# A two-layer hybrid decoder trunk: the RG-LRU recurrence as hand-ordered slots

## The chip, the cores and the metric

The kernel runs on one core of a Trainium2 chip. The metric is the device time of one execution in microseconds (us); a time is the median over its runs. Engines are named as in the profile: PE is TensorE (matrix products; PEld its weight loads), DVE is VectorE, ACT is ScalarE, POOL is GpSimd, SP is SyncE, which here only issues DMAs.

## The reference

One sequence of 1024 positions, width 1024, two layers, float32 throughout. Every layer is `x + gate(c) * mixer(RMSNorm(x) * (1 + scale(c)) + shift(c))`; shift, scale and gate come from one product of silu(c) with `ada_w`. Layer 0 mixes by attention (sliding window of 128 with sinks and relative bias, and forgetting attention). Layer 1 is the Griffin block that most of the change is about:

```python
def rglru_mixer(h, w_in, conv_w, conv_b, w_a, b_a, w_x, b_x, lam, w_out):
    proj = h @ w_in
    xr, gate = proj[..., :LRU_WIDTH], proj[..., LRU_WIDTH:]
    xp = jnp.pad(xr, ((0, 0), (CONV_WIDTH - 1, 0), (0, 0)))      # CONV_WIDTH = 4
    xc = conv_b
    for j in range(CONV_WIDTH):
        xc = xc + xp[:, j:j + S] * conv_w[j]
    # 8 blocks of 128 channels, block-diagonal
    r = sigmoid(einsum('bsnw,nwv->bsnv', xblk, w_a) + b_a)
    i = sigmoid(einsum('bsnw,nwv->bsnv', xblk, w_x) + b_x)
    log_a = -LRU_C * r * softplus(-lam)                           # LRU_C = 8
    a = exp(log_a)
    u = sqrt(-expm1(2.0 * log_a)) * (i * xc)
    # scan over positions: state = a_t * state + u_t
    y = hs * silu(gate)
    return y @ w_out
```

A final RMSNorm ends the trunk.

## The kernel before

Activations stand transposed: 128 channels on the partitions, positions along the free axis, in two halves (h = 0, 1) of 512. Every large product is made in three parts to keep float32 accuracy: weights and activations are each split into a rounded high part (`whi`, `xhi`) and the rest (`wlo`, `xlo`), and `gemm` (line 325) adds whi x xhi, wlo x xhi and whi x xlo in one PSUM bank. A 128-channel output tile of one half is thus 8 x 3 = 24 matrix products of 128x512. Splitting a raw weight half (128x512) is one ACT copy and one POOL subtraction (`split`, line 293); raw halves come by DMA from SP into three buffers.

All instructions go through the helper at line 86, so every row of the profile has L86 and the tiles tell operations apart. A planner outside the kernel orders the instructions of each engine; for engines named in the set `ordered` it keeps the program's order instead. `ordered` holds all engines up to line 609 and PE alone from 610 to line 1298; after that it is empty.

The steps that the change touches, in order of time:
- First norm, second half (lines 508 to 521). `rstd_of` (line 256) makes 1/rms from squares summed on PE into `psq`: DVE and ACT (a Sqrt) make `vb`, and `spread` transposes it on PE into the bank `rs`. `gate_first(i)` takes a gate product out of PSUM (`sg`, a Sigmoid on ACT, then `gy`, a product on DVE).
- Ada products (`mod_steps`, line 542): each is one DVE reduction over a 128x1024 row block that a DMA has brought. Twenty are made with the gates of the second half, two after the last gate, one after each of eight `ps_v` tiles, two at the end.
- `log1p_exp_neg_abs` (line 154), a softplus from Exp and Ln: for the forget gate (line 640), and, at line 1308, for lambda.
- `Chain` (line 1204): the second norm, one object per half: `sums`, `spread` and four `pair`s that write h1 (high and low). Chain 0 is fed in between the products of the first output projection (`ps_o0c`, line 1271), chain 1 in the first lx product (line 1296).
- The recurrence. Channel block c needs the products lx_c (input of the convolution) and lg_c (gate). `use_x` copies lx from PSUM to `xr` and starts `xc`; `recurrence` makes the three other taps on DVE from `xr`, splits `xc` into `xch` and `xcl`, multiplies by the r and i gate matrices (12 products), and makes `th`, `a`, `a2` (in a tile with xcl's tag, so in its buffer), the square root and the scan `hs`; `use_g` gates the result into `y1h`, `y1l`. Program order per c: recurrence(c), lx_{c+2}, lg_c; the planner is free to change it. Outputs alternate between two pairs of PSUM banks (`ps_1`), so a bank comes round every fourth output.
- The second output projection (line 1428) runs its first three tiles over k = 0 to 6 ahead of the last channel's y1.

## Time and profile before

| | |
|---|---|
| median of 3 runs | 904.58 us (901.8 to 905.53) |
| profiled execution | 901.91 us |
| its span, first to last instruction | 900.1 us |
| mean granted clock of TensorE in it | 0.989 |
| busy: PE, DVE, ACT, POOL | 857.3, 599.9, 537.7, 387.8 us |

The page gives busy time by engine, the span in 40 slices and the costliest groups of instructions. In a row of a timeline stand the start in us from the span's first instruction, the duration in us, the engine, the line, the operation, the tiles it writes and reads (`out<-in`), its shape and a count; in square brackets the idle time of the engine ahead of it, and who ended it. Stages, by the tiles: first norm and gates to about 77 us, the rest of the input projections and the attention to about 533, the first output projection to 576, lx, lg and the recurrence to about 812, the second output projection and the final norm to 900.

### The profile page before, as it was taken

To read this page: it belongs to the slowest core of one execution; us is meant where nothing else is said; L and a number is where in the kernel's file an instruction comes from. 1 tells how busy PE (TensorE), PEld (TensorE's weight loads), DVE (VectorE), ACT (ScalarE), POOL (GpSimd) and SP (SyncE) were. 2 spreads that over 40 slices of the span, in tenths; PEclk is the share of its full clock that TensorE was granted. 3 is DMA by queue.
4 is the path that set the end of the run, shared out by engine and by line. 5 is a ranking of instruction groups with operands and counts; after the bars stand their busy time and mean duration, and the time that the engine had idled before them with its cause. 6 is when DMAs were issued, how large, how long until landed. Compare 5 with 4: busy or idle time off the path is not lost.

```text
span 900.1 us, 13512 instructions
## 1 busy us (share of the span) xinstructions
PE 857.3 (95%) x4618; PEld 726.6 (81%) x4618; DVE 599.9 (67%) x1118; ACT 537.7 (60%) x1047; POOL 387.8 (43%) x428
## 2 busy tenths in 40 slices
PE   9999999999999999999989999999999999499995
PEld 8777898888878888888778787788888777387995
DVE  7876797688676565665756677276977788643353
ACT  5745124788676566665756656277757666675332
POOL 4843432343342232332554546353745554686010
PEclk9999999999999999999999999999999999799998
DMA  9944883100013322433464563411111111126042
GB/s 348 403 159 153 275 305 82 49 24 23 26 58 105 121 86 84 125 93 90 143 215 119 161 213 119 131 45 41 42 42 50 53 35 46 35 66 216 1 148 87
DMA packets 54334, 103.84 MB, mean 115 GB/s; under 512 B 6929, under 2 KB 20689, under 8 KB 53497
## 3 DMA queue, kind: packets, MB, share of 16 engines
q1 hardware_dynamic: 53112, 101.93, 34.3%
q10 hardware_dynamic: 1152, 1.05, 0.5%
q8 instruction: 36, 0.59, 0.3%
q14 instruction: 34, 0.27, 0.1%
HBM read 94.02 MB, written 8.93 MB: 114 GB/s over the span
## 4 chain that ended last, share of the span: by engine, by line
PE 64%; DVE 14%; ACT 11%; issue 5%; POOL 3%; DMA 3%; SPq 0%; DVEq 0%; POOLq 0%; ACTq 0%
PE ps_fill L86 21%; PE ps_o L86 8%; PE pst L86 6%; PE ps_o0c L86 5%; PE ps_lx L86 4%; PE oB L86 4%; PE ptB L86 3%; PE sB L86 3%; ACT L86 2%; DVE xc_r L86 2%; DVE ada L86 2%; DVE hs_r L86 2%; DVE th_r L86 2%; PE sA L86 2%; DMA ada<-in_ada_dram 1%
## 5 line engine op out<-in xcount | busy, mean ns | idle before, releaser
L86 DVE TENSOR_TENSOR ptl_B<-ptB,pth_B 128x512 fp32r<-128x512 f32 (+1 forms) x80 | 50.8, 635 | 39.8 <-ACT pth_B L86 39.5
L86 PE MATMUL ps_o<-y1h,wo 128*128 128x256 f32 (+1 forms) x336 | 75.3, 319 | 0.0
L86 ACT ACTIVATE pth_B<-ptB 128x512 fp32r<-128x512 f32 (+1 forms) x80 | 44.1, 552 | 46.0 <-PE ptB L86 45.9
L86 ACT ACTIVATE pB<-pB,mnB 128x128 f32<-128x128 f32 (+3 forms) x64 | 49.6, 774 | 30.7 <-DVE mnB L86 25.2
L86 POOL TENSOR_SCALAR_AFFINE_SELECT pB<-pB 128x128 f32<-128x128 f32 x64 | 19.3, 301 | 94.9 <-DMA pB<-gd 85.8
L86 PEld LDWEIGHTS ps_o<-y1h,wo 128*128 128x128 f32 x336 | 55.9, 190 | 4.6 <-issue 0.3
L86 PE MATMUL pst<-hh,ws 128*128 128x512 f32 x192 | 55.5, 397 | 1.5 <-DVE gy L86 1.5
L86 ACT ACT_TABLE_LOAD x42 | 53.9, 1283 | 1.7 <-PEq L1539 0.7
L86 PE MATMUL ps_o<-y1l,wo 128*128 128x256 f32 (+1 forms) x168 | 53.7, 320 | 0.0
L86 DVE CUSTOM_DVE_ANT_0 ada<-ada,crow,col 128x1024 f32<-128x1024 f32 x32 | 46.0, 1467 | 6.9 <-DMA ada<-in_ada_dram 6.8
L86 PE MATMUL ps_lx<-h1h,wlo_lx 128*128 128x512 f32 x128 | 50.1, 393 | 0.4 <-POOL wlo_lx L86 0.4
L86 PE MATMUL ps_lg<-h1h,wlo_lg 128*128 128x512 f32 x128 | 49.9, 390 | 0.2 <-POOL wlo_lg L86 0.2
L86 PE MATMUL ps_lx<-h1l,whi_lx 128*128 128x512 f32 x128 | 49.9, 391 | 0.0
L86 PE MATMUL ps_lx<-h1h,whi_lx 128*128 128x512 f32 x128 | 49.9, 391 | 0.0
L86 PE MATMUL ps_lg<-h1l,whi_lg 128*128 128x512 f32 x128 | 49.8, 389 | 0.0
L86 PE MATMUL ps_lg<-h1h,whi_lg 128*128 128x512 f32 x128 | 49.8, 389 | 0.0
L86 PE MATMUL ptB<-ident,pB 128*128 128x128 f32 x288 | 45.4, 274 | 3.0 <-DVE gy L86 1.2
L86 PEld LDWEIGHTS ptB<-ident,pB 128*128 128x128 f32 x288 | 35.6, 140 | 14.6 <-ACT pB L86 2.3
L86 DVE CUSTOM_DVE_ANT_0 pB<-sB,pB 128x384 f32<-128x384 f32 (+2 forms) x64 | 35.4, 554 | 17.0 <-PE sB L86 8.0
L86 PEld LDWEIGHTS pst<-hh,ws 128*128 128x128 f32 x192 | 35.7, 188 | 10.9 <-DVE gy L86 1.9
L86 ACT ACTIVATE sq_o<-x 128x512 f32<-128x512 f32 (+1 forms) x33 | 18.0, 547 | 38.1 <-DVE x L86 37.9
L86 DVE SCALAR_TENSOR_TENSOR xc_r<-xr_r,col,xc_r 128x1024 f32<-128x1024 f32 x24 | 37.7, 1582 | 1.3 <-ACT xc_r L86 1.0
(317 smaller groups left out, 2856.5 us busy)
## 6 DMA issues: line engine op xcount, KB each, us to landing
ada<-in_ada_dram SPq DMA_DIRECT2D x36, 512.0 KB
ada<-in_ada_dram SPq DMA_DIRECT2D x6, 1024.0 KB
x<-in_xT_dram SPq DMA_DIRECT2D x20, 256.0 KB
pB<-gd SPq DMA_DIRECT2D x8, 512.0 KB
raw_o0a<-in_wo_dram SPq DMA_DIRECT2D x16, 256.0 KB
raw_o0c<-in_wo_dram SPq DMA_DIRECT2D x16, 256.0 KB
x1d<-x SPq DMA_DIRECT2D x16, 256.0 KB
raw_lx<-in_wl_dram SPq DMA_DIRECT2D x16, 256.0 KB
```

The source lines that it names most:

```text
L86: ins = issue(*args, **kw)
```

## The change

The recurrence becomes a list of slots, one for each channel block, with all engines in program order. lx is no longer copied to `xr`: the taps read the PSUM bank itself, and the three positions that the second half needs of the first are kept in `xt`. Weight halves are loaded one by one (`load_next`) and split a tile at a time (`split_next`). Within a slot the ACT functions are put so that sigmoids and tanh, exp, and sqrt stand together. a2 has a tile of its own and is an ACT square; i x xc moves from POOL to DVE; the cut of `xc` moves from DVE to ACT; the subtraction for the gate matrices moves from DVE to POOL. Before the recurrence: `rstd_of` of the first norm's second half stands after three gates instead of ahead of them, two ada products move into the `ps_v` loop, the softplus of lambda moves to the forget gate's, and the steps of both chains move to later products.

```diff
-    spread = rstd_of(psq, HALF, at, ("ptl", "pth"), "n0_1", ps_t)
     for i in range(3):
         gate_first(i)
+    spread = rstd_of(psq, HALF, at, ("ptl", "pth"), "n0_1", ps_t)
...
-        elif i == 7:
-            mod_steps(2)
...
-        mod_steps(1)
-    mod_steps(2)
+        mod_steps(1 + tb % 2)
...
+    log1p_exp_neg_abs(sp, lam, const, [P, KT], "lm")
...
-            parts = {AT_S: chains[0].sums}
+            parts = {5: chains[0].sums}
         elif e == 2:
-            parts = {0: chains[0].spread, 2: lambda: chains[0].pair(0), 6: lambda: chains[0].pair(2)}
+            parts = {3: chains[0].spread, 5: lambda: chains[0].pair(0)}
         elif e == 3:
-            parts = {2: lambda: chains[0].pair(4), 6: lambda: chains[0].pair(6)}
+            parts = {k: lambda k=k: chains[0].pair(k) for k in (2, 4, 6)}
...
-    ps01.append(proj1(0, "lx_0", 0, w01[0], parts={3: chains[1].sums, 6: chains[1].end}))
-    ps01.append(proj1(1, "lx_1", 0, w01[1]))
+    ps01.append(proj1(0, "lx_0", 0, w01[0], parts={3: chains[1].sums}))
+    ps01.append(proj1(1, "lx_1", 0, w01[1], parts={0: chains[1].end}))
...
+    def split_next():
+        if raws:
+            w = []
+            for _ in range(2):
+                w += half_of(raws.popleft())
+                load_next()
+            ready.append(w)
...
+    def conv(c, h, ps):
+
+        if h == 0:
+            xcs[c], xts[c] = rt("xc", c, bufs=2), rt("xt", c, w=3, bufs=2)
+        xc, o = xcs[c], h * HALF
+        act.activation(xc[:, half(h)], ps, AF.Identity, bias=at_c(C_CB, c), scale=at_c(C_CW + 24, c))
+        if h == 0:
+            copy(xts[c], ps[:, HALF - 3 : HALF])
+
+        def taps():
+            for j in range(3):
+                d = 3 - j
+                parts = [(xc[:, o + d : o + HALF], ps[:, 0 : HALF - d])] + [(xc[:, o : o + d], xts[c][:, 3 - d : 3])] * h
+                for out, src in parts:
+                    dve.scalar_tensor_tensor(
+                        out=out, in0=src, scalar=at_c(C_CW + 8 * j, c), in1=out, op0=ALU.mult, op1=ALU.add
+                    )
+
+        return taps
+
+    def split_xc(c, hs=slice(0, S)):
+        if c not in split_x:
+            split_x[c] = rt("xch", c, F32R), rt("xcl", c, F32R)
+        hi, lo = split_x[c]
+        copy(hi[:, hs], xcs[c][:, hs])
+        sub(dve, lo[:, hs], xcs[c][:, hs], r32(hi[:, hs]))
...
+    def split_r(c):
+        for raw, hi, lo in wrs[c].values():
+            copy(hi, raw)
+            sub(gp, lo, raw, r32(hi))
+
+    def gates(c):
...
+            for h, ps in enumerate(out[t]):
+                for i, (a, b) in enumerate(((whi, xch), (wlo, xch), (whi, xcl))):
+                    mm(ps, a, b[:, half(h)], start=(i == 0), stop=(i == 2))
+        return out
+
+    def gate_a(c, h):
+
+        sg = sgs[c, h] = rp.tile([P, HALF], F32, tag="sg", name=f"sg_r{c}_{h}", bufs=2)
+        act.activation(sg, lgs[c, h], AF.Sigmoid)
+        mul(dve, sg, lgs[c, h], sg)
+        mul(gp, sg, sg, hss[c][:, half(h)])
+
+    def gate_b(c, h):
+        sg = sgs.pop((c, h))
+        copy(y1h[:, c, half(h)], sg)
+        sub(gp, y1l[:, c, half(h)], sg, r32(y1h[:, c, half(h)]))
+
+    lgs, sgs = {}, {}
+    ordered |= ALL
+    for _ in range(3):
+        load_next()
+    load_r(0)
+    for c in range(2):
+        conv(c, 0, ps01[c])()
+    split_xc(0, half(0))
+    split_r(0)
+    taps = conv(0, 1, proj1(0, "lx_0", 1, w01[0]))
+    split_next()
+    taps()
+    split_xc(0, half(1))
+    conv(1, 1, proj1(1, "lx_1", 1, w01[1]))()
+
+    def slot(c):
+        n = c + 2
+        ps = gates(c)
+        if c:
+            gate_a(c - 1, 1)
+        r, i_ = rt("r", c), rt("i", c)
+        for o, t, cb in ((r, "r", C_BA), (i_, "i", C_BX)):
             for h in range(2):
...
+                act.activation(o[:, half(h)], ps[t][h], AF.Sigmoid, bias=at_c(cb, c))
+        th, a_, a2 = rt("th", c), rt("a", c), rt("a2", c)
         act.activation(th, r, AF.Tanh, scale=sp[:, c : c + 1])
+        mul(dve, i_, i_, xcs[c])
+        if c + 1 < KT:
+            load_r(c + 1)
+            split_xc(c + 1)
+        if c:
+            gate_b(c - 1, 1)
         act.activation(a_, r, AF.Exp, scale=nsp[:, c : c + 1])
+        w = ready.popleft()
+        split_next()
+        if n < KT:
+            taps = conv(n, 0, proj1(0, f"lx_{n}", 0, w))
+        act.activation(a2, a_, AF.Square)
+        if n < KT:
+            taps()
         dve.scalar_tensor_tensor(out=th, in0=a2, scalar=1.0, in1=th, op0=ALU.add, op1=ALU.mult)
         act.activation(th, th, AF.Sqrt, bias=tiny)
         mul(dve, i_, i_, th)
         hs_ = hss[c] = rt("hs", c, bufs=2)
         dve.tensor_tensor_scan(out=hs_, data0=a_, data1=i_, initial=0.0, op0=ALU.mult, op1=ALU.add)
+        if n < KT:
+            conv(n, 1, proj1(0, f"lx_{n}", 1, w))()
+            w = ready.popleft()
+            split_next()
+        if c + 1 < KT:
+            split_r(c + 1)
+        lgs[c, 0] = proj1(0, f"lg_{c}", 0, w)
+        gate_a(c, 0)
+        gate_b(c, 0)
+        lgs[c, 1] = proj1(0, f"lg_{c}", 1, w)
...
+    gate_a(KT - 1, 1)
+    gate_b(KT - 1, 1)
+    ordered.clear()
```

## Rows read from the trace of the kernel before

**Rows 1.** The page: busy us and share of each engine; TensorE's granted clock by slice.
```profile
PE 857.3 (95%) x4618; PEld 726.6 (81%) x4618; DVE 599.9 (67%) x1118; ACT 537.7 (60%) x1047; POOL 387.8 (43%) x428
...
PEclk9999999999999999999999999999999999799998
```

**Rows 2.** Table by stage: stretch, length, busy us of each engine, clock, DMA share, GB/s.
```profile
714.60:741.20 26.60, 25.08 (x109) 20.06 (x108) 20.06 (x14) 17.90 (x26) 14.62 (x10) 1.00 0.15 45
...
767.80:790.00 22.20, 10.58 (x39) 7.89 (x38) 15.22 (x11) 16.25 (x24) 13.40 (x9) 0.77 0.12 36
```

**Rows 3.** Waits of PE, whole span: us in total, times, longest.
```profile
PE psr L86 <- DVE xcl_r L86: 14.1, 4, 10.3
...
PE ps_v L86 <- DVE fz L86: 1.4, 1, 1.4
```

**Rows 4.** Timeline of PE, a steady pass.
```profile
715.31 0.39 PE L86 MATMUL ps_lg<-h1h,whi_lg 128*128 128x512 f32 x1
...
725.96 0.39 PE L86 MATMUL ps_lg<-h1l,whi_lg 128*128 128x512 f32 x1
...
728.15 0.50 PE L86 MATMUL psr<-xcl_r,wrh_r 128*128 128x512 f32 x1 [1.35 <-DVE xcl_r L86]
...
733.88 0.50 PE L86 MATMUL ps_lx<-h1h,wlo_lx 128*128 128x512 f32 x1 [0.17 <-POOL wlo_lx L86]
```

**Rows 5.** Timeline of PE, the last channel and the second output projection.
```profile
768.34 0.39 PE L86 MATMUL ps_lg<-h1l,whi_lg 128*128 128x512 f32 x1
...
781.31 0.79 PE L86 MATMUL psr<-xcl_r,wrh_r 128*128 128x512 f32 x1 [10.29 <-DVE xcl_r L86]
...
784.40 0.40 PE L86 MATMUL psi<-xch_r,wrh_r 128*128 128x512 f32 x1
...
812.13 0.50 PE L86 MATMUL ps_o<-y1l,whi_wo 128*128 128x512 f32 x1 [1.23 <-POOL y1l L86]
```

**Rows 6.** Timelines of PE, first norm and both chains of the second.
```profile
59.82 0.72 PE L86 MATMUL pst<-hh,ws 128*128 128x512 f32 x2 [1.52 <-DVE gy L86]
...
543.25 0.66 PE L86 MATMUL rs_n<-ident,vb_n 128*128 128x128 f32 x4 [1.37 <-DVE vb_n L86]
...
584.38 0.63 PE L86 MATMUL rs_n<-ident,vb_n 128*128 128x128 f32 x4 [1.81 <-DVE vb_n L86]
```

**Rows 7.** Timeline of ACT, one pass.
```profile
741.08 1.26 ACT L86 ACTIVATE r_r<-psr,col 128x512 f32<-128x512 f32 x2
...
744.16 1.28 ACT L86 ACT_TABLE_LOAD   x1
745.46 1.15 ACT L86 ACTIVATE a_r<-r_r,nsp 128x1024 f32<-128x1024 f32 x1
...
754.56 0.76 ACT L86 ACTIVATE xc_r<-ps_lx,col 128x512 f32<-128x512 f32 x1
755.23 0.62 ACT L86 ACTIVATE whi_lg<-raw_lg 128x512 fp32r<-128x512 f32 x1
```

**Rows 8.** Groups by shape, 560 to 830 us: busy us, mean ns | idle before.
```profile
L86 POOL TENSOR_TENSOR sg_r<-sg_r,hs_r 128x512 f32<-128x512 f32 x16 | 21.3, 1331 | 16.9 <-DVE sg_r L86 10.4 <-DVE hs_r L86 6.6
...
L86 DVE SCALAR_TENSOR_TENSOR th_r<-xcl_r,th_r 128x1024 f32<-128x1024 f32 x8 | 17.1, 2138 | 0.1
...
L86 DVE TENSOR_TENSOR sg_r<-ps_lg,sg_r 128x512 f32<-128x512 f32 x16 | 11.0, 685 | 14.3 <-POOL wlo_lg L86 13.1 <-ACT sg_r L86 1.2
...
L86 DVE SCALAR_TENSOR_TENSOR x<-ps_o0c,mod,x 128x512 f32<-128x512 f32 x4 | 3.0, 751 | 10.3 <-PE ps_o0c L86 10.3
```

**Rows 9.** Timelines of DVE and POOL, two passes.
```profile
626.07 1.22 DVE L86 SCALAR_TENSOR_TENSOR th_r<-xcl_r,th_r 128x1024 f32<-128x1024 f32 x1
...
635.21 2.28 DVE L86 TENSOR_TENSOR_SCAN hs_r<-a_r,i_r 128x1024 f32<-128x1024 f32 x1
...
729.29 1.30 POOL L86 TENSOR_TENSOR wlo_lx<-raw_lx,whi_lx 128x512 fp32r<-128x512 f32 x1 [3.53 <-ACT whi_lx L86]
729.38 3.35 DVE L86 TENSOR_TENSOR_SCAN hs_r<-a_r,i_r 128x1024 f32<-128x1024 f32 x1
```

More of the change, by code (lines that the diff above doesn't have):

```diff
@@ L24 @@
 RUN = 32
-AT_S = 5
 P = 128
@@ L641, in hybrid_trunk @@
     dve.scalar_tensor_tensor(out=lf, in0=z, scalar=0.0, in1=lf, op0=ALU.min, op1=ALU.subtract)
+    sp, nl, nsp = (const.tile([P, KT], F32, name=n) for n in ("sp", "nl", "nsp"))
+    lam = col[:, C_LAM : C_LAM + 8]
+    log1p_exp_neg_abs(sp, lam, const, [P, KT], "lm")
+    dve.tensor_scalar(out=nl, in0=lam, scalar1=-1.0, scalar2=0.0, op0=ALU.mult, op1=ALU.max)
+    add(dve, sp, sp, nl)
+    dve.tensor_scalar(out=nsp, in0=sp, scalar1=-8.0, scalar2=None, op0=ALU.mult)
+    dve.tensor_scalar(out=sp, in0=sp, scalar1=8.0, scalar2=None, op0=ALU.mult)
     gd = dram.tile([8, NB, S], F32, name="gd")
@@ L1320, in hybrid_trunk @@
         jobs_l += [(c + 2, f"lx_{c + 2}")] * (c + 2 < KT) + [(8 + c, f"lg_{c}")]
-    jobs_l = collections.deque(jobs_l)
-    ready = collections.deque()
-    def next_weights():
-        if jobs_l:
-            ready.append(load_tile(wl[jobs_l[0][0]], jobs_l[0][1]))
-            jobs_l.popleft()
-    def proj_l(name, use):
-        next_weights()
-        w = ready.popleft()
-        for h in range(2):
-            use(h, proj1(0, name, h, w))
+    halves = collections.deque((ti, i, name) for ti, name in jobs_l for i in range(2))
@@ L1361, in load_r @@
             sync.dma_start(raw, src[:, c])
-            wrs[c][t] = rt("wrh", c, F32R, w=P, bufs=2), rt("wrl", c, F32R, w=P, bufs=2)
-            copy(wrs[c][t][0], raw)
-            sub(dve, wrs[c][t][1], raw, r32(wrs[c][t][0]))
-    def recurrence(c):
-        xr, xc = xrs[c], xcs[c]
-        for j in range(3):
-            dve.scalar_tensor_tensor(
-                out=xc, in0=xr[:, j : j + S], scalar=col[:, C_CW + 8 * j + c : C_CW + 8 * j + c + 1], in1=xc,
-                op0=ALU.mult, op1=ALU.add,
-            )
-        xch, xcl = rt("xch", c, F32R), rt("xcl", c, F32R)
-        dve.tensor_copy(xch, xc)
-        sub(dve, xcl, xc, r32(xch))
-        ri = []
-        for src, cb, t in ((wa, C_BA, "r"), (wx, C_BX, "i")):
-            whi, wlo = wrs[c][t]
-            o = rt(t, c)
-            for h in range(2):
-                hs = slice(h * HALF, (h + 1) * HALF)
-                ps = (ps_s if t == "r" else ps_t)(f"ps{t}_{c}_{h}")
-                for i, (a, b) in enumerate(((whi, xch), (wlo, xch), (whi, xcl))):
-                    pe.matmul(ps, a, b[:, hs], start=(i == 0), stop=(i == 2))
-                act.activation(o[:, hs], ps, AF.Sigmoid, bias=col[:, cb + c : cb + c + 1])
-            ri.append(o)
-        r, i_ = ri
-        th, a_, a2 = rt("th", c), rt("a", c), rt("xcl", c)
-        act.activation(th, r, AF.Tanh, scale=sp[:, c : c + 1])
-        act.activation(a_, r, AF.Exp, scale=nsp[:, c : c + 1])
-        mul(dve, a2, a_, a_)
@@ new lines, in load_r @@
+            wrs[c][t] = raw, rt("wrh", c, F32R, w=P, bufs=2), rt("wrl", c, F32R, w=P, bufs=2)
+    def split_r(c):
[3 more added lines that the diff above has]
+    def gates(c):
+        out = {}
+        for t, ps_ in (("r", ps_s), ("i", ps_t)):
+            _, whi, wlo = wrs[c][t]
+            xch, xcl = split_x[c]
+            out[t] = [ps_(f"ps{t}_{c}_{h}") for h in range(2)]
+            for h, ps in enumerate(out[t]):
+                for i, (a, b) in enumerate(((whi, xch), (wlo, xch), (whi, xcl))):
+                    mm(ps, a, b[:, half(h)], start=(i == 0), stop=(i == 2))
+        return out
@@ L1398, in recurrence @@
         dve.tensor_tensor_scan(out=hs_, data0=a_, data1=i_, initial=0.0, op0=ALU.mult, op1=ALU.add)
-    def use_g(c):
-        def use(h, ps):
-            hs = slice(h * HALF, (h + 1) * HALF)
-            sg = rp.tile([P, HALF], F32, tag="sg", name=f"sg_r{c}_{h}", bufs=2)
-            act.activation(sg, ps, AF.Sigmoid)
-            mul(dve, sg, ps, sg)
-            mul(gp, sg, sg, hss[c][:, hs])
-            copy(y1h[:, c, hs], sg)
-            sub(gp, y1l[:, c, hs], sg, r32(y1h[:, c, hs]))
-        return use
-    for c in range(2):
-        use = use_x(c)
-        use(0, ps01[c])
-        use(1, proj1(c, f"lx_{c}", 1, w01[c]))
-    next_weights()
-    load_r(0)
-    for c in range(KT):
-        recurrence(c)
-        if c + 1 < KT:
-            load_r(c + 1)
-        if c + 2 < KT:
-            proj_l(f"lx_{c + 2}", use_x(c + 2))
-        proj_l(f"lg_{c}", use_g(c))
+        if n < KT:
[8 more added lines that the diff above has]
+        lgs[c, 1] = proj1(0, f"lg_{c}", 1, w)
+    for c in range(KT):
+        slot(c)
+    gate_a(KT - 1, 1)
+    gate_b(KT - 1, 1)
+    ordered.clear()
     l1.close()
```

34 lines of the change are left out of this document (10 added, 24 removed).

## The prediction

> **What bounds the kernel now.** I read the busy table and the slices first. TensorE (PE) is busy for 857.3 of 900.1 us, and its clock stands at full speed in all slices but two [rows 1], so only what makes PE wait, or makes it run at less than full speed, can move the end. In a dense stretch a 128x512 product follows the last one after (725.96 - 715.31) / 47 = 0.2266 us [rows 4]; that is my yardstick, and a larger step between two products is a loss. The table by stage then shows the recurrence. One pass of its loop (channels 1 to 5) needs 48 products of lx, 48 of lg and 12 of the r and i gates: 108 x 0.2266 = 24.5 us. The stretch of 26.6 us in [rows 2] is such a pass, with DVE at 20.1, ACT at 17.9 and POOL at 14.6 us: no engine beside PE is full, so the 2.1 us above the yardstick are order, not work. The last passes are far worse: from 767.8 to 790.0 PE is busy for 10.6 of 22.2 us, at a mean clock of 0.77 [rows 2].
>
> The waits of PE name the place: 14.1 us on DVE's xcl, 10.3 us of it in one piece [rows 3]. I then went through PE's own rows in order of time. A row gives the wait; the loss against the yardstick is 0.15 to 0.3 longer, for the restart:
> - rstd chains: rs_n at 543.25 waits 1.37 (loss 1.5) and at 584.38 1.81 (loss 2.1) [rows 6]
> - steady passes: the xcl product at 728.15 waits 1.35 (loss 1.5), and POOL's wlo at 733.88 costs 0.35 [rows 4]. Three passes have both (around 701, 728 and 755); together 5.3 us
> - last channel: from 768.34 to 781.31 PE makes three steps in 12.97 us, 12.3 too many, 10.29 of them one wait on xcl; then seven steps to 784.40 take 3.09 us for 1.59, at the lower of the two clocks (1.2 GHz) [rows 5]. Loss 13.8
> - the output projection waits 1.23 for y1l at 812.13 (loss 1.4) [rows 5].
> Two losses lie earlier: 1.52 us of waiting before pst at 59.82 (loss 1.7), on a bank that a gate product of DVE frees [rows 6], and 1.4 us of ps_v on DVE's fz [rows 3]. Sum of all: 27.2 us. That is the most the change can win, because it adds no product and removes none.
>
> **The change part by part.** All sums are against the profiled execution (901.9 us, 1.8 us of them outside the span); the median of the runs shown, 904.58, is 2.7 above it.
>
> *Gates of the first norm (lines 511 to 513).* The three gate steps now stand ahead of the rstd chain, in a time in which ACT and DVE wait for the sums, so the bank of pst at 59.82 is free early. The six products ahead of `spread` last 1.36 us, and the chain ends by then; nothing is late next. A further table load (1.28 us [rows 7]) falls ahead of gates 3 to 7, where PE has its own products. Bounds -1.7 to +1.3; I take -1.5, near the wait's row.
>
> *Ada products.* Twelve products after the gates stay twelve; two leave the place ahead of the first ps_v eviction for the turns of tb = 1, 3, 5, 7. The wait on fz can go (-1.6) or move to a later turn, since DVE's order is not given there. Bounds -1.6 to +1.5; I take -0.7. The softplus of lambda moves to that of the forget gate: 128x8 instructions beside PE's fill products, taken at nothing. If the scheduler does not share their tables it costs two loads of 1.28 on ACT, and decay's transposes could wait for that.
>
> *Chain 0.* `spread` goes from k = 0 to k = 3 of product 2: nine products, 2.0 us, cover the 1.5 us. The pairs end later, but the first consumer is lx_0, four products of 24 away. -1.5 (bounds -1.5 to 0).
>
> *Chain 1.* `end` goes six products later: 1.36 of the 2.1 us are covered. What is late next are the h1 halves for lx_0's second half, which now follow `spread` by 21 products instead of 27; that can give back up to 1.36. I take -1.0.
>
> *Entry to the slots.* Gates of channel 0 now come after only 96 lx products, where the scheduler had put them after lx_2. On DVE two sets of three taps, a split, three taps and a split stand in line: some 9 x 0.69 + 2 x 0.6 = 7.4 us from the end of chain 1's pairs. By the same count PE gets there about a microsecond earlier. +1.3 (bounds 0 to 4).
>
> *Slots 1 to 5.* PE's own order needs only things made a slot earlier: xch, xcl and the gate matrices of c+1 are split in slot c, a2 has a buffer of its own and no longer shares xcl's, lg's weights are split about 2 us before they are used, and banks come round every fourth product. So PE runs at 24.5 us unless the other engines' loop is longer. I add that loop in ACT's given order, from a slot's first sigmoid, with pitches from [rows 7] (an instruction starts up to 0.1 us before the end of the last): sigmoids to 3.3 (the last waits for its product), tanh 1.17, split 1.05, y1h 0.53, load 1.30, exp 1.17, two weight copies 1.04, conv and tail 0.87, square 1.1: 11.5 us. DVE's three taps read PSUM like the eviction of 0.75 us [rows 8] and end at 12.2; then th 1.22 [rows 9], sqrt 1.15, product 1.22, scan 2.28 [rows 9]: 18.1; three taps with three small tails 2.4, sg 0.69, POOL 1.33 [rows 8], y1h 0.53: 22.9 us, when nothing collides. A DVE instruction with two SBUF operands does collide with POOL: the scan takes 2.28 undisturbed, but 3.35 where POOL's 1.30 us began just before it [rows 9], and th has a mean of 2.14 against 1.22 [rows 8, 9]; sg, which reads PSUM, has 0.685 as its mean beside POOL [rows 8]. Six instructions of the loop are open to this (th, product, scan, three tails): ceiling 22.9 + 6 x 1.33 = 30.9. I take 24.5, one whole collision and a bit, since half the weight splits fall on the scan; that equals PE's need, and of 5.3 us lost 1.0 stays: -4.3. For totals, ACT has about 20 us per slot (3 table loads for 4, no xr copy, but the square and xch's split), DVE 15, POOL 11: all under 24.5. SP moves the same megabyte per slot, three halves ahead.
>
> *Slots 6 and 7.* Without lx products PE has only 13.6 us in slot 6, but wrh of channel 7 now stands behind the sqrt on ACT (about 14.5 by the sums above) and wrl behind the scan on POOL (about 18.1). Gates 7 end near 19.3 instead of 16.3: 3.0 us lost (bounds 1 to 6), for 13.8: -10.8. After them PE has 48 lg and 63 projection products, 25 us; the chain to y1l (sigmoids, tanh, exp, sqrt, scan, gate) is some 19 to 22 us, so the wait of 1.4 goes: -1.4.
>
> Sum: -1.5 - 0.7 - 1.5 - 1.0 + 1.3 - 4.3 - 10.8 - 1.4 = -19.9, so 882.0 in a profiled execution like this one, and 904.6 - 19.9 = 885 us as the median.
>
> **The rivals.** *Half of it comes back.* Gates 7 wait like before, because the tail is one chain of ACT and DVE in either order (10 of the 13.8 us stay), or the entry costs 4. For it: the chain's instructions are all still there. Against it: xcl's own reason, the shared buffer, is gone. Gain 6 to 14, near 894.
>
> *The slot's loop becomes the bound.* ACT may not start a slot's sigmoids before y1h of the slot before. With the loop at its ceiling of 30.9, six slots lose 6 x 6.4 = 38 us more: 923. It decides above 24.5 + 20 / 6 = 27.8 us per slot: from there on the kernel is slower than before. For it: fixed order cannot step round a collision, and the scan is hit in most passes now. Against it: POOL has less to do per slot.
>
> *A dearer table load.* Three loads stand in the loop. If each held ACT for twice its 1.28 us [rows 7], the loop would be 24.5 + 3 x 1.28 = 28.3 us, and six slots would lose 23 us: 908. Against it: exp starts 0.02 us after its load's end [rows 7], so 2 in 100. The Trainium skill, "ScalarE: Activation LUTs", section "What ACT_TABLE_LOAD costs", states a drain of about 1380 ns behind every load, with which the loop would be 28.6 us and the time 910; this trace does not show that drain.
>
> *The change doesn't do what it says.* New tiles lie over those of the attention, and the given order lets one late release hold a whole queue; then the entry eats what the slots win: 904.
>
> **How the numbers follow.** My forecast, a gain of 15 to 26 us (879 to 890), has 0.65; half back 0.17; nothing moved 0.08; the loop or the dearer load 0.10. Faster by over 0.5%: 0.82; within 0.5% (4.5 us, about what a measurement of this kernel can tell from no change): 0.08; slower: 0.10. The range goes from 877, all 27.2 us gone, to 900, the end of the second case; the last two cases, 0.18, are left out.
>
> **What would show it right or wrong.** In PE's waits the entry for psr on DVE's xcl should be gone, one for psr on POOL's wrl of about 3 us should stand there, and rs_n should be under 2 us in all. Passes of the loop should last 24.5 us, with the first matrix product of each slot on time; ACT should have three table loads in each. A pass above 26.6, with ACT waiting for POOL's sg ahead of y1h and PE waiting for lg's wlo or for a bank, would make the prediction wrong. So would a wait of over 5 us at the first gates or at gates 7.

## The result, and the profile after

The changed kernel takes 896.37 us in the median of six runs (894.64 to 899.41), the kernel before 903.91 us on the same chip (six runs, 901.8 to 905.53): a ratio of 0.9919, with an interval of 0.9899 to 0.994. That is 7.5 us faster, where 19.9 were forecast; the time lies inside the range of 877 to 900, near its slow end. The profiled execution of after took 896.32 us (span 894.5, mean clock 0.986). Before's own, 901.91, lay 2.0 us under its median, so the two traces differ by 5.6 us of span and not by 7.5.

The page, answering to [rows 1]: busy by engine, and the granted clock by slice.

```profile
PE 862.2 (96%) x4618; PEld 731.6 (82%) x4618; DVE 563.4 (63%) x1143; ACT 537.6 (60%) x1051; POOL 378.3 (42%) x428
...
PEclk8999999999999999999999999999999999999998
```

The dip of the clock at the last channel has gone from its slice. The table by stage (length, busy us of each engine, clock, DMA share, GB/s) answers to [rows 2] in its first two rows; the other rows are the second projection's start and two stretches of half pace.

```profile
705.30:729.80 24.50, 24.50 (x109) 20.23 (x108) 14.62 (x16) 17.62 (x25) 13.54 (x11) 1.00 0.15 49
767.80:790.00 22.20, 20.16 (x87) 15.80 (x86) 7.83 (x6) 15.66 (x23) 17.04 (x12) 1.00 0.17 54
790.00:817.00 27.00, 22.12 (x89) 17.24 (x88) 9.64 (x11) 15.55 (x25) 18.75 (x15) 0.94 0.57 185
606.80:610.50 3.70, 3.70 (x11) 2.88 (x10) 2.52 (x7) 3.69 (x6) 0.00 (x0) 0.54 0.05 14
812.60:815.20 2.60, 2.60 (x7) 1.99 (x6) 2.11 (x4) 2.57 (x6) 0.00 (x0) 0.51 1.01 347
```

A pass of the loop is now full: 24.50 of 24.50 us against 25.08 of 26.60. The last channel's stretch holds 87 products instead of 39. But the stretch behind it, from 790 to 817, is not: PE is busy for 22.12 of 27.00 us. PE's waits answer to [rows 3]:

```profile
PE ps_o L85 <- DVE x L85: 2.7, 1, 2.7
PE rs_n L85 <- DVE vb_n L85: 2.3, 2, 1.8
PE psr L85 <- ACT xch_r L85: 1.9, 1, 1.9
PE ps_v L85 <- DVE fz L85: 1.4, 1, 1.4
PE ps_o L85 <- DVE sg_r L85: 1.2, 1, 1.2
...
PE ps_v L85 <- POOL wvl L85: 1.1, 1, 1.1
...
PE ps_o L85 <- ACT y1h L85: 0.9, 1, 0.9
PE psr L85 <- POOL wrl_r L85: 0.9, 1, 0.9
PE psi L85 <- POOL wrl_r L85: 0.7, 1, 0.7
```

The 14.1 us on xcl are gone. In their place stand one wait at the first gates (`xch_r`), small ones at gates 7 (`wrl_r`; 0.43 more on `wrh_r`), and three of the second projection that weren't there: on `sg_r`, on `y1h` and on `x`. (Of the 2.3 us of rs_n, 1.8 is the final norm's, which before had as well.) PE's timeline, answering to [rows 5] and to the entry: the first gates, gates 7 and the tail.

```profile
605.76 0.50 PE L85 MATMUL psr<-xch_r,wrh_r 128*128 128x512 f32 x1 [1.88 <-ACT xch_r L85]
...
607.98 0.63 PE L85 MATMUL psi<-xch_r,wrh_r 128*128 128x512 f32 x1
...
768.73 0.50 PE L85 MATMUL psr<-xch_r,wrh_r 128*128 128x512 f32 x1 [0.43 <-ACT wrh_r L85]
...
770.11 0.50 PE L85 MATMUL psr<-xch_r,wrl_r 128*128 128x512 f32 x1 [0.88 <-POOL wrl_r L85]
...
772.50 0.50 PE L85 MATMUL psi<-xch_r,wrl_r 128*128 128x512 f32 x1 [0.73 <-POOL wrl_r L85]
...
795.57 0.73 PE L85 MATMUL ps_o<-y1h,wo 128*128 128x512 f32 x2 [1.21 <-DVE sg_r L85]
...
801.57 0.50 PE L85 MATMUL ps_o<-y1h,whi_wo 128*128 128x512 f32 x1 [0.95 <-ACT y1h L85]
...
812.07 1.22 PE L85 MATMUL ps_o<-y1h,wo 128*128 128x512 f32 x2 [2.72 <-DVE x L85]
813.09 0.63 PE L85 MATMUL ps_o<-y1l,wo 128*128 128x512 f32 x1
```

Each row's wait is 0.15 to 0.3 us shorter than its loss against 0.2266 us a product, as before. The three tail waits lose 1.4, 1.1 and 2.9 us; before lost 1.4 in all there. Soon after the waits at 605.76 and 812.07 (from 607.55 and 812.66 on) six or seven products follow each other after 0.43 us, about twice the yardstick, and the granted clock of the stretches above is 0.54 and 0.51, near the 1.2 GHz level.

Why x is late at 812.07 stands on SP and DVE:

```profile
764.99 42.74 SPq L85 DMA_DIRECT2D raw_wo<-in_wo_dram  x15
807.83 9.41 SPq L85 DMA_DIRECT2D x<-x1d  x16
```

```profile
811.26 2.12 DVE L85 SCALAR_TENSOR_TENSOR x<-ps_o,mod,x 128x512 f32<-128x512 f32 x3 [8.46 <-DMA x<-x1d]
```

SP issues fifteen halves of wo, which wait for raw buffers, before the first residual input. DVE can empty the three tiles made ahead only when that has landed, and PE's fifth tile needs such a bank.

### The profile page after: what moved, and what is told of

It is laid out like the page before. It is cut to its first block, busy times and chain, and to the rows that moved or that the text cites. A ratio compares the mean times of both kernels' runs of the same rounds, so it can differ in the third digit from the quotient of the medians.

```text
span 894.5 us, 13516 instructions
## 1 busy us (share of the span) xinstructions
PE 862.2 (96%) x4618; PEld 731.6 (82%) x4618; DVE 563.4 (63%) x1143; ACT 537.6 (60%) x1051; POOL 378.3 (42%) x428
## 4 chain that ended last, share of the span: by engine, by line
PE 62%; DVE 12%; ACT 11%; issue 5%; POOL 4%; DMA 4%; SPq 0%; DVEq 0%; POOLq 0%; ACTq 0%
PE ps_fill L85 21%; PE ps_o L85 8%; PE ps_o0c L85 5%; PE pst L85 5%; PE oB L85 4%; PE ptB L85 3%; PE sB L85 3%; DVE xc_r L85 3%; DMA ada<-in_ada_dram 2%; DVE hs_r L85 2%; PE ps_lx L85 2%; DVE ada L85 2%; PE sA L85 2%; PE oA L85 1%; PE ptA L85 1%
## 5 line engine op out<-in xcount | busy, mean ns | idle before, releaser
L85 DVE SCALAR_TENSOR_TENSOR xc_r<-ps_lx,col,xc_r 128x509 f32<-128x509 f32 (+2 forms) x48 | 35.6, 744 | 23.2 <-ACT xt_r L85 22.1
```

The lines of the kernel that those rows point to most:

```text
L85: ins = issue(*args, **kw)
```

## The experiments

All are the changed kernel with one edit, unless said otherwise; ratios are against the kernel before on the same chip.

| run | median us | ratio, interval |
|---|---|---|
| small_only (before + early edits) | 902.04 | 0.9977, 0.9962 to 0.9992 |
| slots_only (after - early edits) | 897.55 | 0.9926, 0.9904 to 0.9947 |
| sp_late | 897.2 | 0.9913, 0.9891 to 0.9935 |
| x_early | 889.01 | 0.9838, 0.9817 to 0.986 |
| bank | 892.32 | 0.9857, 0.9837 to 0.9876 |
| wo_dve | 895.86 | 0.9895, 0.9877 to 0.9912 |
| tail_order | 889.07 | 0.9836, 0.9813 to 0.9859 |
| early_r | 893.58 | 0.9887, 0.9864 to 0.9911 |
| entry_r | 898.21 | 0.9933, 0.9911 to 0.9955 |
| best | 892.21 | 0.9869, 0.9848 to 0.9889 |
| act_plus | 899.13 | 0.994, 0.9919 to 0.9962 |
| chain7 | 891.14 | 0.9847, 0.983 to 0.9865 |
| chain7b | 888.3 | 0.9827, 0.9812 to 0.9842 |
| warm (one run) | 894.33 | none |

**The tail: residual inputs (x_early).** The first three tiles of x get buffers of their own, whose loads SP can issue long before.

```diff
+    xs = [y1p.tile([P, HALF], F32, name=f"xs_{e}") for e in range(AHEAD)]
-            sync.dma_start(xn[:, e], x1d[:, h, e, o : o + tw])
+            sync.dma_start(xs[e] if t0 == 0 and e < AHEAD else xn[:, e], x1d[:, h, e, o : o + tw])
```

> The changed kernel with the residual inputs of the first three output tiles in three tiles of their own, so that their loads need not stand behind the fifteen loads of wo on SP. Theory A (order on SP's queue): the products at 812.07 no longer wait 2.72 us for DVE's residual; the gain against the changed kernel is 3.2 us (2.9 and the restart), near 893.2; the waits of ps_o at 795.57 (1.21) and 801.57 (0.95) stay. Rival B (the residual has other reasons, its DMA or POOL's and ACT's order): a wait of over 1.5 us stays at that product, time 895 to 896.4. Rival C: the three loads hold SP at the entry to the slots and a new wait of PE of over 1 us appears between 600 and 660 us.

Measured: the wait at 812.07 and its half-pace products are gone, PE's losses from gates 7 to the end fall from 10.0 to 5.7 us. The ratio falls by 0.0081, some 7 us, and its interval is apart from after's. 4.3 us of that are the tail's. This execution is also 2.8 us sooner at the first gates (602.92 against 605.76), where nothing was edited: 0.8 us sooner at 440 us already, and from 440 to 460 it made 105 products at a clock of 1.00, where after made 94 at 0.91. Whether the other executions of this run differ from after's in the same way isn't shown, so of the 7 us only the tail's 4.3 are put down to the edit. PE's timeline behind gates 7, all waits of the tail:

```profile
792.73 0.73 PE L85 MATMUL ps_o<-y1h,wo 128*128 128x512 f32 x2 [1.24 <-DVE sg_r L85]
...
798.83 0.50 PE L85 MATMUL ps_o<-y1h,whi_wo 128*128 128x512 f32 x1 [1.04 <-ACT y1h L85]
```

The waits on sg and y1h stay, so the DMA order is a cause by itself.

**The tail: the third tile's bank (bank).**

```diff
-            ps = ps_1(f"ps_o1_{t0}_{e}")
+            ps = (ps_s if t0 == 0 and e == 2 else ps_1)(f"ps_o1_{t0}_{e}")
```

> The changed kernel with the third output tile in a bank of ps_s, which the r gates left, instead of the bank of lg's first half in channel 7. Theory A: the wait at 795.57 for DVE's sg (1.21 us, loss 1.38) is gone, but PE then stands 1.4 us longer at the last channel's y1h (801.57: 0.95 becomes 2.3), since y1h comes when ACT and POOL bring it; the banks come round one tile later, so the product that waited 2.72 us at 812.07 for DVE's residual takes a bank that was free at 802.8: gain 3.2 us, near 893.2. Rival B: only the first wait counts and nothing comes back at y1h: gain 1.4 to 4.6. Rival C: the residual's wait only moves to a later tile and the 1.4 us are lost again at y1h: no gain, 896.4.

The wait on sg_r is gone: it was one for a bank that the last gate step frees. Two other things happened. PE reached y1h sooner and waited longer there, and seven products behind it ran at half pace; and the wait on x went too, since its bank was now needed later. The losses from gates 7 on fall by 2.9 us (3.2 were expected); the ratio falls by 0.0062, some 5.6 us, with an interval apart from after's, and what the rest is isn't shown.

```profile
801.82 0.80 PE L85 MATMUL ps_o<-y1h,whi_wo 128*128 128x512 f32 x1 [2.53 <-ACT y1h L85]
...
802.84 2.52 PE L85 MATMUL ps_o<-y1h,wo 128*128 128x512 f32 x6
```

**The tail: weight splits on DVE (wo_dve).** Seven of the fourteen low halves of wo go from POOL to DVE.

```diff
-                        split(raw, *(t[:, (e - 1) % 4, 4 * c : 4 * c + 4] for t in wr))
+                        split(raw, *(t[:, (e - 1) % 4, 4 * c : 4 * c + 4] for t in wr), (gp, dve)[c])
```

> The changed kernel with seven of the fourteen lo halves of wo (tiles 1 to 7, second halves) made on DVE, which is idle for 15 of 27 us there, instead of POOL, which is busy for 23 of 27. Theory A: POOL brings the last channel's sg (798.46) 1.3 to 2.6 us earlier and raw buffers come free earlier, so the wait for y1h at 801.57 (0.95, loss 1.1) goes: gain 1.1 us there; the loads behind wo on SP come earlier too, so that the wait of 2.72 us at 812.07 shrinks: 1 to 4 us in all, 892.5 to 895.3. Rival B: ACT's y1h stands behind copies that wait for the loads of wo, whoever makes the lo halves: the wait at y1h stays, gain under 0.5 us. Rival C: DVE's extra work delays the scan or sg and the wait at 795.57 grows by over 1 us: slower than the changed kernel.

The y1h wait went (one of 0.18 us on y1l is left), but sg_r waited 1.81 at 797.08 and x 2.04 at 812.17: 0.7 us less loss from gates 7 on (9.3 for 10.0), a result between the theories, and the intervals overlap. In this trace POOL's load was part of y1h's lateness, not of the wait on sg_r.

**The tail written out (tail_order).** x_early, and the last slot in an order of its own: both halves of lg_7 ahead of the sqrt, wo's first tile split ahead of the last sigmoids, three more wo halves behind the square, the gate steps straight behind the scan.

```diff
+        if last:
+            for h in range(2):
+                lgs[c, h] = proj1(0, f"lg_{c}", h, w)
+            wo_tiles(1)
+            for _ in range(3):
+                split_wo()
...
+    gate_a(KT - 1, 0)
+    split_wo()
+    gate_b(KT - 1, 0)
```

> The changed kernel with the residual inputs of three output tiles in tiles of their own (as in the run with early loads), and with the last slot written out with the work of the output projection in it: both halves of lg ahead of the sqrt, wo's first tile split ahead of the last sigmoids, three halves of wo behind the square, both gates straight behind the scan. Theory A: the three losses of the tail were order, not work: sg is ready at about 793 and y1h by 796, so the waits at 795.57 (1.21) and 801.57 (0.95) go as well as the one at 812.07 (2.72) with its slow products: 1.4 + 1.1 + 4.4 = 6.9 us less than the changed kernel, near 889.5; against the run with early loads 2.5 less. Rival B: the last channel's chain is bound by its own length (sigmoids to y1l some 19 us): a wait of over 1.5 us for y1h stays, gain as with early loads alone, 4.4. Rival C: halves of wo come later and PE waits for wo by over 1 us between 785 and 812.

No wait of PE is left between gates 7 and the final norm. The table of 768 to 815 in three kernels: after, x_early, tail_order.

```profile
768.00:815.00 47.00, 40.08 (x165) 31.33 (x164) 15.88 (x15) 29.05 (x44) 35.79 (x26) 0.97 0.36 114
```

```profile
768.00:815.00 47.00, 43.98 (x191) 35.39 (x191) 16.45 (x18) 29.23 (x44) 33.80 (x25) 1.00 0.38 123
```

```profile
768.00:815.00 47.00, 44.95 (x196) 36.58 (x196) 20.55 (x18) 30.10 (x46) 32.34 (x24) 1.00 0.39 125
```

In the same time PE makes 31 more products than in after. Its median equals x_early's; the last 2 to 3 us of the tail can't be told apart in the times, only in the trace.

**The early edits and the slots apart (small_only, slots_only).** The edits outside the recurrence (gates of the first norm, ada turns, softplus, chains 0 and 1) on the kernel before; and the changed kernel with them undone.

```diff
-    spread = rstd_of(psq, HALF, at, ("ptl", "pth"), "n0_1", ps_t)
...
+    spread = rstd_of(psq, HALF, at, ("ptl", "pth"), "n0_1", ps_t)
...
-        mod_steps(1)
-    mod_steps(2)
+        mod_steps(1 + tb % 2)
...
-            parts = {0: chains[0].spread, 2: lambda: chains[0].pair(0), 6: lambda: chains[0].pair(2)}
+            parts = {3: chains[0].spread, 5: lambda: chains[0].pair(0)}
```

> The kernel before with the five small edits of the change (gates ahead of the first norm's chain, ada steps, softplus of lambda in const, chain 0, chain 1) and the recurrence as it was. Theory A (what the trace of the changed kernel shows): the two chains give 2.7 us, and the early edits give nothing or cost up to 1.8: DVE's row of ada products begins when ACT brings the five gates' sigmoids, and in the new order these stand behind one more table load (74.63, 1.28 us), so the 1.8 us won at 60 us are waited off at ps_v. Together -2.7 to -0.9 us, ratio 0.997 to 0.999. Forecast of the prediction: -1.5 - 0.7 - 1.5 - 1.0 = -4.7 us, ratio 0.995. Rival: the softplus at the start costs its whole 3 us and all is paid on: slower than before by 0 to 1.5 us, ratio 1.000 to 1.002.

> The changed kernel with the five small edits undone: only the slots, their convolution from PSUM and the split of weights half by half are left. Theory A (terms of the changed kernel's trace): the slots win 5.3 us in the passes and 11.2 at gates 7 and lose 3.7 at the entry and 5.9 in the tail: -6.5 to -7 us, ratio 0.9925. Theory B (the small edits are worth the forecast 4.7 us): the slots alone give only 2.8 us, ratio 0.997. Forecast of the prediction for this part: +1.3 - 4.3 - 10.8 - 1.4 = -15.2, ratio 0.983.

The early edits alone win 2.1 us, the slots alone 6.7: they add up, within their intervals, to the whole. As the chains win 2.8 us in small_only's trace, the edits ahead of them cost about 0.7, which with the interval of the 2.1 can be anything from a gain of 0.6 to a cost of 2.1. In slots_only, whose early part is in before's order, PE waits 1.32 us at 115.01 on POOL's wvl, which waits for a load; the profile of before had no such wait, and all fifteen others have it. So the forecast rested, in this stage, on an execution in which that load came early.

**The softplus (sp_late).** In after, ACT begins with four table loads where before had two (at 0.73 and 3.85), since nothing holds the softplus of lambda back once its input is there:

```profile
0.73 1.28 ACT L85 ACT_TABLE_LOAD   x1 [0.73 <-PEq L1583]
...
3.38 1.28 ACT L85 ACT_TABLE_LOAD   x1
...
4.91 1.28 ACT L85 ACT_TABLE_LOAD   x1
...
6.42 1.28 ACT L85 ACT_TABLE_LOAD   x1
```

The first squares start at 7.82 instead of 5.25, the first product of the projections at 19.98 instead of 16.93. (Over all traces it is 18.78 to 21.31 in the twelve with four loads, 16.93 to 18.28 in the four with two.) This run makes lambda's copy depend on the forget gate's result.

```diff
-    lam = col[:, C_LAM : C_LAM + 8]
+    lam = const.tile([P, KT], F32, name="lam")
+    dve.scalar_tensor_tensor(
+        out=lam, in0=lf[:, 0], scalar=0.0, in1=col[:, C_LAM : C_LAM + 8], op0=ALU.mult, op1=ALU.add
+    )
```

> The changed kernel with lambda's softplus tied behind the forget gate's lf (it reads a copy of lambda that is made from lf), so that its two extra table loads can no longer stand at the start. Theory A: the start is worth what PE loses there, 3.05 us at its products near 16.9 us, but the load of wv (ACT's wvh waits for it until 110.45) and DVE's fz bind PE again at ps_v, so that the 1.8 us which the reordered gates win at 60 us are taken back there: PE stands 0.0 +- 0.4 us against the kernel before at 130 us (the changed kernel +1.8), and the gain is 1.8 us, near 894.6. Rival B: the whole 3.0 us stays, PE stands -1.2 against the kernel before at 130 us, near 893.4. Rival C: swallowed by other waits, PE at +1.4 or more at 130 us, time as the changed kernel, 896.4. In all of them the table loads of ACT before 10 us fall from four to two.

The start is back (two loads, first product at 17.35), and the time is not: PE waits 2.32 at 114.56 for POOL's wvl, and 2.44 at 151.53 for `kla`, behind two further table loads at 145.94 and 147.94. What was won was waited off, as rival C has it.

**Gates 7 and the entry (early_r, entry_r).** early_r loads the gate matrices a slot earlier and splits them right behind xch; entry_r has this and also puts the first half of lx_2 ahead of gates 0.

```diff
+    load_r(1)
...
-            load_r(c + 1)
+            split_r(c + 1)
...
-        if c + 1 < KT:
-            split_r(c + 1)
+        if c + 2 < KT:
+            load_r(c + 2)
```

> The changed kernel with the gate matrices of the next channel loaded a slot earlier and split right behind xch, instead of behind the sqrt on ACT and the scan on POOL. Theory A: gates 7 (768.73, 770.11 and 772.50, losses 0.59, 1.15 and 0.90) no longer wait; the 2.6 us come out at the end only as far as the tail lets them: the last channel's chain starts 2.6 us earlier too, and the loads of wo on SP stay where POOL's splits put them, so 1 to 2.6 us, 893.8 to 895.4. Rival B: gates 7 still wait, for the banks that the sigmoids of slot 6 leave: no gain. Rival C: the earlier loads stand ahead of lx and lg halves on SP and a pass becomes longer than 24.6 us: slower.

> The run with early gate matrices, and at the entry the first half of lx_2 (24 products) ahead of the gates of channel 0. Theory A: the wait on xch (loss 2.04) goes, and with it the nine to ten products at half the pace that follow it (0.20 each, 1.7 in all): gates 0 begin 5.4 us later and find everything ready, the gates of channel 1 do not wait because their matrices are split early, PE is 3.7 us ahead at 631 us; the end gains as much as the tail lets through, 1 to 3.7 us against 893.6. Rival B: the gates of channel 1 wait instead (the work of slot 0 starts 1.8 us later on ACT): PE only 0 to 2 us ahead at 660 us. Rival C: the slow products do not hang on the wait; 2.0 us ahead and as many slow products as before.

In early_r gates 7 have no wait at all, and PE then waits 4.14 us on sg_r instead of 1.21: the chain to y1 is no earlier. The last scan starts 189.6 us behind the first gate product in both kernels, since the loop of ACT and DVE now takes 24.87 us from one first sigmoid to the next instead of 24.57. The time can't be told from after's (the intervals overlap).

```profile
793.47 1.22 PE L85 MATMUL ps_o<-y1h,wo 128*128 128x512 f32 x2 [4.14 <-DVE sg_r L85]
```

In entry_r the first gates don't wait either, but PE is at lg_0 before its weights are split (1.65 at 618.42 on ACT, 0.85 at 619.77 on POOL, nine products at half pace), and the tail waits 5.15 on sg_r. Its ratio is 0.0046 above early_r's. best, with all mendings so far and the softplus moved to some 565 us, lost its gain in the same way (892.2 us, where 882 to 883 were expected): 1.65 on ACT's whi_lg at 616.77, and in the tail 1.25 on ACT's wo at 786.93 and the wait of this row:

> All together: the tail written out with early residual inputs, gate matrices early, lx_2 ahead of gates 0, and lambda's softplus behind a residual of the output projection's second half (some 565 us, where ACT and DVE are busy for a third of the time). Theory A, the parts add up from the losses of PE in the traces: 889.1 with the written out tail, less 2.6 at gates 7, less 3.7 at the entry, less 0 to 1 for the start: 882 to 883, ratio 0.976. Rival B: the tail's chain cannot follow PE that comes 6 us earlier, and waits of 2 to 5 us come back at the bank of the third output tile or at y1h, as in the run with early gate matrices alone: 885 to 888. Rival C: the softplus costs its 2 us at its new place as well: 884 to 885.

```profile
788.80 0.68 PE L85 MATMUL ps_o<-y1h,wo 128*128 128x512 f32 x1 [1.36 <-POOL wo L85]
```

**The chain of the last slot (chain7, chain7b).** So the bound there may be ACT's chain; two runs ask. chain7 (tail_order and early_r) takes the first y1h of channel 6 out of the way of the last sigmoids; chain7b takes the second out of the way of the last exp as well.

```diff
         if last:
+            gate_b(c - 1, 0)
+            split_next()
+            gate_a(c - 1, 1)
...
+            gate_b(c - 1, 1)
```

> The written out tail and the early gate matrices together, and in the last slot y1h of (6, 0) behind the tanh instead of ahead of the sigmoids, wo's first tile behind it. In the run with all parts together gates 7 were done at 769.8 but the first sigmoid of slot 7 came at 778.44, behind a y1h that waited 3.65 us for POOL and two copies of wo, and PE then waited 3.1 us for wo's next halves. Theory A (ACT's given order across slots 6 and 7 is what holds the tail once gates 7 are early): the sigmoids start 4 to 6 us earlier, no wait of over 1 us stands between gates 7 and the last norm, and the 2.66 us at gates 7, which the written out tail still lost, come out at the end: 889.1 - 2.7 = 886.4, ratio 0.980. Rival B: wo's halves are late by SP's loads (three raw buffers), so PE waits 2 to 5 us for them as in the run with all parts: 889 to 892. Rival C: the last channel waits elsewhere (POOL's sg): y1h again over 1.5 us late, 888 to 890.

> The run before this one with one move: y1h of (6, 1), which waited 4.62 us for POOL's sg ahead of the exp of channel 7 (781.66), now stands behind the square and the first two halves of wo. Theory A (only ACT's given order holds the tail): exp starts at about 778.5 instead of 783.61, wo's first halves are copied 4 us earlier, the waits of PE for wo (losses 1.18 and 1.63) and for sg (1.56) go, and the time falls by 3 to 4.4 us to 887 to 888, ratio 0.980 to 0.981. Rival B: wo's halves wait for SP's loads, and PE's two waits for wo stay over 1 us in all: 890 to 891. Rival C: the chain's later links collide with POOL's halves of wo: sg or y1h waits of over 1.5 us, 889 to 890.

In chain7 the sigmoids began at 770.82 instead of 778.44 (best), but y1h then waited 4.62 us for POOL ahead of exp, and the waits on wo stayed (1.02, 1.35). In chain7b exp starts at 777.41 instead of 783.61, and of the tail's waits 0.87 on sg_r and 0.24 on wo are left. It has the lowest time of all, 888.3 us (one run at 885.49), but x_early and tail_order lie in its interval. So ACT's order is what held the exp, in the trace; that it is worth time is not shown.

**The slot's loop (act_plus).** The square is done three times: 2.1 us more ACT in each slot, to see whether the loop or PE sets a pass.

```diff
-        act.activation(a2, a_, AF.Square)
+        for _ in range(3):
+            act.activation(a2, a_, AF.Square)
```

> The changed kernel with the square of each slot computed three times: 2.1 us more on ACT in the middle of the slot's chain; nothing else differs. Theory A (the loop of ACT and DVE is as long as PE's 24.5 us, with some 0.2 us to spare, and only the order of the queues couples it to PE): the first sigmoid falls behind PE by 1.9 to 2.1 us more in each slot; PE itself has nearly a slot to spare and keeps its 24.57 us for some slots, but the last channel is 8 to 14 us late: gates 7 or the tail wait that long, 904 to 910. Rival B (the loop has over 2.1 us to spare, the floor of 22.9 of the prediction): no pass changes and the time stays within 1 to 3 us of the changed kernel. Rival C (PE follows the loop at once): passes of 26.4 to 26.7 us, PE waiting in each, 908 to 912.

Four passes of PE stayed at 24.57 us (gates at 629.1, 653.7, 678.3, 702.8, 727.4), the fifth took 25.1. The loop itself became longer: from a slot's first sigmoid to the next it takes 25.41 us, where after has 24.57.

```profile
681.54 1.26 ACT L85 ACTIVATE r_r<-psr,col 128x512 f32<-128x512 f32 x2
...
706.95 1.26 ACT L85 ACTIVATE r_r<-psr,col 128x512 f32<-128x512 f32 x2
```

Of the 2.1 us, 1.26 fill a wait of ACT for DVE's th ahead of the sqrt (its row in after, at 719.21, is shown below), and the other 0.84 lengthen the loop: it had nothing to spare. PE, which needs only things made a slot earlier, keeps its pace until that lead is used up. Over six slots the loop takes 4.6 us more than in after, and the price comes at gates 7, where PE waits 5.0 us longer:

```profile
772.55 0.79 PE L85 MATMUL psr<-xch_r,wrh_r 128*128 128x512 f32 x1 [5.44 <-ACT wrh_r L85]
```

This is theory A, with 0.84 us a slot for its 1.9 to 2.1. Of the 5.9 us more that are lost at gates 7, 4.3 were given back by shorter waits behind. The ratio is 0.0021 above after's, about 2 us and inside the intervals, where more was expected.

**Half pace after a wait (warm).** Eight products that nothing reads fill PE's wait at the first gates.

```diff
+                if c == 0 and t == "r" and h == 1:
+                    fill = ps_t("fill")
+                    for _ in range(8):
+                        mm(fill, whi, xch[:, half(0)], start=True, stop=True)
```

> The changed kernel with eight products into a bank that nobody reads, ahead of the second half of gates 0, where PE otherwise waits 1.9 us for xch (605.76). Theory A (the half pace follows from PE standing still for about 2 us): PE waits under 0.4 us there, and the products behind it follow each other at 0.2266 us; gates 0 begin as late as before (xch sets it), and lx_2's products come 1.5 to 1.8 us earlier. Rival B (the pace has another cause at this place): seven or more of the next twelve products still take 0.43 us each.

```profile
603.44 1.99 PE L85 MATMUL fill<-xch_r,wrh_r 128*128 128x512 f32 x8
605.52 0.50 PE L85 MATMUL psr<-xch_r,wrh_r 128*128 128x512 f32 x1
...
606.58 0.39 PE L85 MATMUL psi<-xch_r,wrh_r 128*128 128x512 f32 x1
```

The gate products follow at 0.23 us. It is one execution, and chain7b had the whole wait (1.90) without slow products behind it: over 604.20 to 608.40 its clock was 1.00.

```profile
604.20:608.40 4.20, 4.20 (x17) 3.19 (x18) 3.28 (x7) 4.17 (x6) 0.00 (x0) 1.00 0.11 39
```

So filled time helps is likely, not shown.

## Why the prediction was half right

The direction and most of the signs that it named came true: no wait on xcl, a wait on wrl_r (1.6 us, where about 3 were named), passes of 24.5 with three table loads. rs_n should have been under 2 us in all and was 2.3; 1.8 of that is the final norm's, which the change doesn't touch, and the chains have 0.4. The sum did not come true. The pair of traces, in its own steps (found: how much later PE is, after against before, at the same number of products):

| step | forecast | found |
|---|---|---|
| gates of the first norm, ada, softplus | -2.2 | +1.7 |
| attention at 440 to 446 (not in the sum) | 0 | +1.8 |
| chain 0 | -1.5 | -1.5 |
| chain 1 | -1.0 | -0.8 |
| entry to the slots | +1.3 | +4.1 |
| slots 1 to 5 | -4.3 | -5.7 |
| gates 7 | -10.8 | -10.9 |
| after gates 7 | -1.4 | +5.6 |
| sum | -19.9 | -5.7 (spans: -5.6) |

The large steps were read well. At the chains, 547.30 has no wait and 586.36 has 0.43; a wait on h1l at 595.81 gives back 0.4 us, as the forecast said it might. The loop has the pitch of 24.57 that the forecast took, one first sigmoid to the next (24.8 in the first two slots), with a scan that collides with POOL's split (3.42 us). A table load is followed by its first function at once: the load at 711.48 takes 1.28 us, and exp starts at 712.77. The Trainium skill, "ScalarE: Activation LUTs", section "What ACT_TABLE_LOAD costs", states a drain of about 1380 ns behind each load; this row shows none.

```profile
706.43 1.26 ACT L85 ACTIVATE r_r<-psr,col 128x512 f32<-128x512 f32 x2
...
711.48 1.28 ACT L85 ACT_TABLE_LOAD   x1
712.77 1.15 ACT L85 ACTIVATE a_r<-r_r,nsp 128x1024 f32<-128x1024 f32 x1
...
719.21 1.15 ACT L85 ACTIVATE th_r<-th_r,tiny 128x1024 f32<-128x1024 f32 x1 [1.26 <-DVE th_r L85]
...
731.00 1.26 ACT L85 ACTIVATE r_r<-psr,col 128x512 f32<-128x512 f32 x2
```

So neither loop rival came. But the loop is just as long as PE's pass: act_plus and early_r lengthen it (25.41 and 24.87), and the price shows at gates 7 or behind them, not in PE's passes.

*The step that failed is the last one*: "the chain to y1l ... is some 19 to 22 us, so the wait of 1.4 goes". The chain was longer than PE's 25 us of work beside it. From the end of gates 7 (773.93) to the end of the first y1l (803.62) it took 29.7 us, and 27.6 to y1h. The figure had been the links of the slot's loop added up (sigmoids, tanh, exp, sqrt, scan, gate), with no term for the halves of wo that ACT and POOL split between these links, nor for the loads that those halves wait for:

```profile
776.23 0.63 ACT L85 ACTIVATE y1h<-sg_r 128x512 fp32r<-128x512 f32 x1 [4.40 <-POOL sg_r L85]
...
777.25 1.26 ACT L85 ACTIVATE r_r<-psr,col 128x512 f32<-128x512 f32 x2
...
800.37 0.63 ACT L85 ACTIVATE wo<-raw_wo 128x512 fp32r<-128x512 f32 x1 [1.00 <-DMA raw_wo<-in_wo_dram]
800.91 0.61 ACT L85 ACTIVATE y1h<-sg_r 128x512 fp32r<-128x512 f32 x1
```

```profile
793.86 4.64 POOL L85 TENSOR_TENSOR wo<-raw_wo,wo 128x512 fp32r<-128x512 f32 x3 [3.55 <-ACT wo L85]
798.46 1.29 POOL L85 TENSOR_TENSOR sg_r<-sg_r,hs_r 128x512 f32<-128x512 f32 x1
```

The first sigmoid comes 3.3 us behind gates 7, after a y1h of channel 6 that waits for POOL; POOL's sg starts 2.9 us after DVE's is done, behind three halves of wo. In tail_order, with the same links in another order, the chain takes 23.0 us to y1l, and no wait is left.

The step also asked about one operand, y1l, and named nothing else that would be late: a bank under sg_r, and x's loads behind fifteen wo loads on SP. Gates 7 ending 11 us sooner put PE 11 us sooner at everything behind. Of the 7.1 us lost there, 2.7 lie at sg_r and y1h and 4.4 at x, with the half pace behind it. Of the 14.2 us by which the two sums differ, 7.0 lie in this step, and tail_order's trace has 7.1 us less loss in this stretch than after's: shown. That the gain at gates 7 is partly handed on and not kept is shown by early_r, entry_r and act_plus, in which a wait moves between gates 7 and sg_r.

*The entry was mis-sized*: 4.1 us for 1.3. The forecast counted DVE's line, by which PE would be early by about a microsecond; ACT's xch, which ends the wait, made it 2.04, and the slower products behind it 2.0. It lies at the upper bound given (0 to 4). Moving PE's work alone did not mend it in entry_r.

*The early steps* won nothing near 2.2 us. The wait on the bank is gone (60.71 has none), but the wait on fz is the same 1.43 us in both traces, so the ada term of -0.7 did not come. A further table load falls ahead of the next gates (1.28 us at 74.63); the forecast saw it and gave it PE's products as cover, and PE did not wait there. The softplus was "taken at nothing"; it stood in an unordered part, where its instructions went first of all, and the first product of the projections starts 3 us later. What decides at 115 us is the load of wv: in fifteen of the sixteen traces PE waits on wvl, and the product that waits starts between 113.29 and 116.00, with two table loads at the start as with four. Only before's trace has it at 112.90, without a wait. So the +1.7 is what this pair of executions shows, and over medians the steps ahead of the chains come to about +0.7, not clear of nothing. What sets the landing of that load is open.

*The 1.8 us at 440* are no part of the change. The first product of attention group B's output, oB, starts 1.7 us later than in before (273.2 against 271.5), the last 3.5 (523.7 against 520.2). The same wait of about 1.6 us on ptl_B stands in all sixteen traces; in after's execution, and in five others, PE went at half pace behind it, in before's it did not: bad luck of this pair. (From 440 to 460 its clock was 0.91, with 94 products; before's 1.00, with 108.)

Of the rivals, "half of it comes back" named the right size (a gain of 6 to 14) with two causes: gates 7, which did not wait as before, and an entry of 4, which did come. The reason that it gave for gates 7, a tail that is one chain of ACT and DVE in either order, comes near what held PE for 2.7 us behind gates 7. The largest single loss, the wait on x, was in no rival.

## What to carry to other kernels

When a stall of 10 us goes, everything behind it is wanted 10 us earlier: list for each of the next consumers its operands, its bank and the DMA queue in front of its loads, and not the one wait that the old trace shows. A load that is free early should be issued ahead of loads that wait for buffers; here that single move took 4.3 us out of the tail, more than half of what the whole change had won. A wait removed in one slot of an order by hand can come back further on, as in early_r and best, where the chain that feeds it has not become shorter too. And a sum of a chain's links holds only if nothing else is put between them: count the other work that the same engines are given there.

## What the runs showed of the hardware that was not expected

- A wait of PE of about 2 us cost up to twice its length. Behind the entry's wait (loss 2.04 to 2.08) some six to eight products ran at 0.43 us instead of 0.23, in nine of the ten traces that have it, 1.4 to 1.6 us more than in the tenth, chain7b; behind the x wait (loss 2.7 to 3.0) in after, warm, sp_late and entry_r, but not in slots_only (2.92). Behind losses of 1.0 to 1.7 us in the recurrence and the tail most traces show none; best, with two such waits 1.9 us apart, does, and chain7, with two much like them as far apart, does not.
- It is not the same from run to run: the wait at 440 (about 1.6 us in all sixteen traces) had it in six, and chain7b had none at its entry. At up to 1.8 us a place, executions with the same waits differ by it.
